# Second parts of feed-forward weights and activations: accumulating transfers in place of GpSimd subtractions

## The chip, the cores and the metric

The kernel runs on one core of a Trainium2 chip. The metric is the device time of one execution in microseconds (us); lower is better. The engines named below are TensorE (PE, with its weight load PEld), VectorE (DVE), ScalarE (ACT), GpSimd (POOL) and SyncE (SP, which issues transfers).

## The reference, cut to what matters

One inference step of a one-layer decoder trunk on 512 prompt rows and 64 sample rows, 576 tokens in all, with a model width of 1024. A token mixing part (a chunked state space recurrence beside a delta-rule recurrence) comes first. The change lies in the feed-forward block behind it:

```python
h = h + mix
hf = rmsnorm(h, w['norm_ffn'])
h = h + (jax.nn.silu(hf @ w['w_gate']) * (hf @ w['w_up'])) @ w['w_down']
gate = jax.nn.sigmoid(rmsnorm(h, w['norm_ple']) @ w['w_ple_gate'])
h = h + gate * (p.astype(h.dtype) @ w['w_ple_proj'])
```

All data are float32, and `D_FF` is 2816, which is 22 tiles of 128 columns.

## The kernel before, in words

**Two parts for every operand.** The matmuls take operands of a rounded float32 type. So every weight tile and every activation tile is kept as a first part `hi`, its rounded copy, and a second part `lo = source - hi`. A product is then formed as three matmul groups: hi by hi, hi by lo, lo by hi. `split` (L185) makes the two parts of a tile in SBUF, `wsplit` (L197) loads a weight tile of 128 x 512 from HBM into `raw` first. In both, ACT writes `hi` with a copy, and DVE or GpSimd writes `lo` with a subtraction (L194, L206). Which of the two does it is told by `lo_eng`, by `only`, or by a counter `flip` that alternates between GpSimd and DVE.

**Buffers.** `raw` has three buffers, `whi` and `wlo` of `wsplit` have two each (pool `wp`). A buffer of `raw` is free when its second part has been formed; one of `whi` or `wlo` when PE has done the matmuls that read it.

**The feed-forward stage** (L1355 on) goes over the 22 column tiles in eleven pairs.
- Pair one (loop `for f in range(2)`) uses plain linear layers: `linear` (L225) reads a tile of four 128-row weight blocks with `wload` and issues 24 matmuls of 288 columns for it (four blocks, two halves of the tokens, three groups). With the order `WLAST` the second part of the weight comes last.
- Pairs two to eleven (loop `for p in range(1, NFF // 2)`, p from 1 to 10) form the gate projection of both tiles with seven block products in place of eight (`gate_pair`, L1411). It loads the weight blocks a11, a21, a22 and a12, forms the sums s1, s2 and s4 on DVE (tile `sw`) and one difference on GpSimd (L1418), and calls `product` (L1399) seven times. Each `product` splits its weight into `wh` and `wl` (three buffers each) and issues twelve matmuls: first part by both parts of the activation, then second part by the first part. The results are put together by DVE (L1431, L1437, L1440) and GpSimd (L1429, L1434, L1435), and go through Silu on ACT.
- For each tile of a pair an up projection follows (`linear`, two weight tiles), DVE multiplies it onto the gate, and `inner` splits the result into `ah` and `al`, the activations of the down projection.
- After pair six (p = 5) and after pair eleven (p = 10) `down` (L1446) multiplies what has been collected by `w_down`: eight `linear` calls of three weight tiles each, whose results DVE scales and GpSimd adds to `h` (L1452).

The activation operands T1 to T4 of the block products are formed once, ahead of pair two (L1375 to L1388), by DVE, ACT and GpSimd.

**The order.** Each engine runs its instructions in the order in which they were laid out when the program was built; a planner that simulates the times of the instructions (`schedule_with_timeline_sim=True`) chooses that order, starting from the order of the source. SP issues all weight loads, in order too. The kernel before issues no transfer from GpSimd.

Of the kernel before, what the change touches and what calls it, by code (L numbers as in the profile page):

```python
# [8 lines left out]
F32 = mybir.dt.float32  # L9
F32R = mybir.dt.float32r  # L10
AF = mybir.ActivationFunctionType
ALU = mybir.AluOpType
# [63 lines left out]
def hybrid_step(ctx, tc, A):  # L76
# [2 lines left out]

    cp = ctx.enter_context(tc.tile_pool(name="cp", bufs=1))  # L80
    wp = ctx.enter_context(tc.tile_pool(name="wp", bufs=2))
    xp = ctx.enter_context(tc.tile_pool(name="xp", bufs=8))
    lin = ctx.enter_context(tc.tile_pool(name="lin", bufs=2, space=PSUM))
    dp = ctx.enter_context(tc.tile_pool(name="dp", bufs=1, space=DRAM))
# [3 lines left out]
    def nm(s):  # L88
        uid[0] += 1
        return f"{s}_{uid[0]}"  # L90

    def act(out, in_, func=AF.Copy, scale=1.0, bias=0.0):
        return S.activation(out, in_, func, bias=bias, scale=scale)  # L93
# [87 lines left out]
    wat = [0]  # L181
    flip = [0]
    only = [None]

    def split(src, pool, tags, shape, lo_eng=None, hi=None, lo=None, hi_eng=None, **kw):  # L185
        hi = hi if hi is not None else pool.tile(shape, F32R, tag=tags[0], name=nm(tags[0]), **kw)
        lo = lo if lo is not None else pool.tile(shape, F32R, tag=tags[1], name=nm(tags[1]), **kw)
        if hi_eng:
            hi_eng.tensor_copy(hi[:], src)
        else:  # L190
            act(hi[:], src)
        flip[0] += 1
        eng = lo_eng or (G if flip[0] % 2 else V)
        eng.tensor_tensor(lo[:], src, hi[:].bitcast(F32), ALU.subtract)  # L194
        return hi, lo

    def wsplit(src, n, hi=None, lo=None):  # L197
        raw = wp.tile([P, 512], F32, tag="raw", name=nm("raw"), bufs=3)
        nc.sync.dma_start(raw[:, 0:n], src)
        if hi is None:  # L200
            hi = wp.tile([P, 512], F32R, tag="whi", name=nm("whi"))
            lo = wp.tile([P, 512], F32R, tag="wlo", name=nm("wlo"))
        act(hi[:, 0:n], raw[:, 0:n])
        flip[0] += 1
        eng = only[0] or (G if flip[0] % 2 else V)
        eng.tensor_tensor(lo[:, 0:n], raw[:, 0:n], hi[:, 0:n].bitcast(F32), ALU.subtract)  # L206
        return hi, lo

    ahead = []
# [1136 lines left out]

    XF = st["x"]
    AF2 = []

    def inner(s_):  # L1350

        f = len(AF2)
        AF2.append(split(s_[:], fp, (f"ah{f}", f"al{f}"), [P, NT], lo_eng=G))

    for f in range(2):  # L1355
        ps = lin_ps()
# [42 lines left out]
    def product(ps, w, n, first, eng):  # L1399
        hi, lo = split(w[:], cm, ("wh", "wl"), [P, 512], lo_eng=eng, bufs=3)  # L1400
        for p, q in WLAST:
            for k in range(4):
                T.matmul(ps, (hi, lo)[p][:, k * P:(k + 1) * P], OPS[n][k][q], start=first and p == q == k == 0,  # L1403
                         stop=p == 1 and k == 3, skip_group_check=True)
# [6 lines left out]
    def gate_pair():  # L1411
# [10 lines left out]
        sa, sb = ft("sa"), ft("sb")  # L1422
        product(a, a11, "B11", True, V)
        p1 = kept(a)
        product(b, s2, "T2", True, G)
        p6 = kept(b)
        product(c, s1, "T1", True, V)
        p5 = kept(c)
        G.tensor_tensor(p6[:], p6[:], p1[:], ALU.add)  # L1429
        product(a, a12, "B21", False, G)  # L1430
        V.tensor_tensor(sa[:, N1], a, rs[:, N1], ALU.mult)  # L1431
        product(b, a21, "T3", False, V)
        p67 = kept(b)
        G.tensor_tensor(p67[:], p67[:], p1[:], ALU.add)  # L1434
        G.tensor_tensor(sb[:, N2], p67[:], p5[:], ALU.add)  # L1435
        product(c, s4, "B22", False, G)
        V.tensor_tensor(sa[:, N2], c, p6[:], ALU.add)  # L1437
        V.tensor_tensor(sa[:, N2], sa[:, N2], rs[:, N2], ALU.mult)
        product(b, a22, "T4", False, V)
# [15 lines left out]
        AF2.clear()  # L1455

    for p in range(1, NFF // 2):
        for s_ in gate_pair():
            up = lin_ps()
            linear(XF, up, WLAST)  # L1460
            V.tensor_tensor(s_[:], up, s_[:], ALU.mult)
            inner(s_)
        if p == NSPLIT - 1:
            down(False)
# [208 lines left out]
```

## Time and profile before

| | us |
|---|---|
| median of three runs | 1341.91 |
| lowest, highest | 1338.66, 1345.79 |
| span of the profiled execution | 1349.0 |

The profile is of one execution, and its page gives its span, from the first to the last instruction, and no other time for it. A row of the profile names the engine, the operation, the tile written and the tiles read ("wlo<-raw,whi" is the second part of a weight tile, "al<-sa,ah" that of an activation), the count, the busy time in us and the mean of one in ns. "Idle before" is the time in which the engine stood still ahead of these instructions, and what ended it. A view by stretches of time gives each engine's busy time in the stretch, the clock that was granted to PE (1.00 is full speed) and the share of time in which the 16 DMA engines were busy.

### The profile page before, as it was taken

Reading aid. Unit: us, or ns where it says so; the run is one execution under the profiler, and the core shown is the slowest. Engines: PE = TensorE matmul, PEld = TensorE weight load, DVE = VectorE, ACT = ScalarE, POOL = GpSimd, SP = SyncE. Lnnn points to the kernel's source line nnn. Section 1 sums busy time; section 2 is a strip of 40 time slices with the busy share of each in tenths; the row PEclk is TensorE's granted clock in tenths of the full one; section 3 lists DMA queues with packets and bytes.
Section 4 is the critical chain, followed back from the end, with each engine's and each line's share of the span. In section 5 each row is a group of like instructions: output and inputs, shape, how many; then the busy total and the mean of one; then the engine's idle time right before and its main releaser. Section 6 shows DMA issues by size and latency. Waiting matters only on the chain.

```text
span 1349.0 us, 26596 instructions
## 1 busy us (share of the span) xinstructions
PE 1246.8 (92%) x10525; PEld 1150.7 (85%) x10525; DVE 826.0 (61%) x1443; ACT 618.9 (46%) x1256; POOL 625.6 (46%) x597
## 2 busy tenths in 40 slices
PE   6897999999989978899999969989999999999997
PEld 6787897889868957788779859889999999999997
DVE  6648666887687785943466667886553135443454
ACT  6565436534654463343434364464442124433363
POOL 5425413642355154122456645565654336654642
PEclk9897799899979978889989989998999999999998
DMA  5322242234232412262454542222323222314322
GB/s 164 125 68 66 77 117 63 85 103 116 75 99 78 109 41 80 94 214 83 157 176 131 179 125 72 73 93 88 92 88 87 79 86 82 93 59 149 96 89 71
DMA packets 94461, 135.58 MB, mean 100 GB/s; under 512 B 34705, under 2 KB 39057, under 8 KB 94337
## 3 DMA queue, kind: packets, MB, share of 16 engines
q1 hardware_dynamic: 93760, 133.36, 32.4%
q8 instruction: 83, 1.36, 0.4%
q10 hardware_dynamic: 576, 0.52, 0.1%
q14 instruction: 42, 0.34, 0.1%
HBM read 106.10 MB, written 27.75 MB: 99 GB/s over the span
## 4 chain that ended last, share of the span: by engine, by line
PE 63%; DVE 14%; ACT 4%; issue 4%; DMA 3%; POOL 3%; DVEq 0%; SPq 0%; ACTq 0%; POOLq 0%
PE lin L234 21%; PE lin L1403 8%; PE lin L223 6%; PE lin L221 6%; PE lin L222 6%; DVE h L395 2%; PE lin L1508 1%; PE lin L1509 1%; PE lin L1510 1%; DVE tmp L674 1%; DVE wlo L206 1%; DVE Tt L676 1%; PE lin L613 1%; PE cx L797 1%; DVE suv L831 1%
## 5 line engine op out<-in xcount | busy, mean ns | idle before, releaser
L206 POOL TENSOR_TENSOR wlo<-raw,whi 128x512 fp32r<-128x512 f32 (+1 forms) x108 | 146.4, 1356 | 352.5 <-ACT whi L93 269.5
L93 ACT ACTIVATE whi<-raw 128x512 fp32r<-128x512 f32 (+1 forms) x232 | 143.3, 618 | 259.1 <-PE lin L234 126.4
L221 PE MATMUL lin<-xhi,whi 128*128 128x288 f32 (+1 forms) x784 | 243.3, 311 | 2.5 <-ACT whi L93 2.2
L223 PE MATMUL lin<-xhi,wlo 128*128 128x288 f32 (+1 forms) x784 | 241.5, 308 | 2.3 <-POOL wlo L206 2.3
L222 PE MATMUL lin<-xlo,whi 128*128 128x288 f32 (+1 forms) x784 | 241.5, 308 | 0.3 <-POOL xlo L194 0.3
L206 DVE TENSOR_TENSOR wlo<-raw,whi 128x512 fp32r<-128x512 f32 (+1 forms) x124 | 100.9, 814 | 103.2 <-PE lin L234 60.4
L221 PEld LDWEIGHTS lin<-xhi,whi 128*128 128x128 f32 (+1 forms) x784 | 151.0, 193 | 9.3 <-ACT whi L93 2.6
L223 PEld LDWEIGHTS lin<-xhi,wlo 128*128 128x128 f32 (+1 forms) x784 | 150.7, 192 | 6.2 <-POOL wlo L206 2.8
L222 PEld LDWEIGHTS lin<-xlo,whi 128*128 128x128 f32 (+1 forms) x784 | 150.8, 192 | 4.8 <-issue 1.2
L234 PE MATMUL lin<-xhi,whi 128*128 128x288 f32 x384 | 62.3, 297 | 3.2 <-ACT xhi L93 3.0
L234 PE MATMUL lin<-xlo,whi 128*128 128x288 f32 x384 | 60.8, 298 | 0.0
L234 PE MATMUL lin<-xhi,wlo 128*128 128x288 f32 x384 | 59.3, 297 | 0.0
L234 PEld LDWEIGHTS lin<-xhi,whi 128*128 128x128 f32 x384 | 54.6, 189 | 3.8 <-ACT xhi L93 1.7
L234 PEld LDWEIGHTS lin<-xlo,whi 128*128 128x128 f32 x384 | 54.8, 191 | 0.0
L234 PE MATMUL lin<-ah,wlo 128*128 128x288 f32 x352 | 54.7, 296 | 0.0
L234 PE MATMUL lin<-al,whi 128*128 128x288 f32 x352 | 54.7, 296 | 0.0
L234 PE MATMUL lin<-ah,whi 128*128 128x288 f32 x352 | 54.7, 296 | 0.0
L234 PEld LDWEIGHTS lin<-xhi,wlo 128*128 128x128 f32 x384 | 54.3, 191 | 0.0
L1403 PE MATMUL lin<-T,wh 128*128 128x288 f32 x320 | 50.1, 296 | 4.5 <-DVE T L194 2.8
L674 DVE TENSOR_TENSOR tmp<-L,Tt 72x30 f32<-72x30 f32 (+14 forms) x120 | 49.2, 410 | 3.2
L234 PEld LDWEIGHTS lin<-ah,whi 128*128 128x128 f32 x352 | 49.6, 189 | 0.0
L234 PEld LDWEIGHTS lin<-ah,wlo 128*128 128x128 f32 x352 | 49.6, 189 | 0.0
(425 smaller groups left out, 3197.8 us busy)
## 6 DMA issues: line engine op xcount, KB each, us to landing
raw<-wts SPq DMA_DIRECT2D x271, 256.0 KB, 2.6
S<-s_wkv SPq DMA_DIRECT2D x8, 512.0 KB, 5.1
hd<-s_ssm SPq DMA_DIRECT2D x8, 512.0 KB, 4.5
o_ssm_s<-hd SPq DMA_DIRECT2D x8, 512.0 KB, 2.9
xbc_d<-E SPq DMA_DIRECT2D x12, 288.0 KB, 2.1
x<-xT SPq DMA_DIRECT2D x8, 288.0 KB
gate_d<-g SPq DMA_DIRECT2D x8, 288.0 KB, 2.5
bv_d<-rw SPq DMA_DIRECT2D x8, 288.0 KB
```

What stands on the lines that cost most here:

```text
L93: return S.activation(out, in_, func, bias=bias, scale=scale)
L206: eng.tensor_tensor(lo[:, 0:n], raw[:, 0:n], hi[:, 0:n].bitcast(F32), ALU.subtract)
L221: T.matmul(ps[:, a:b], whi, xhi[:, a:b], start=first, stop=False)
L222: T.matmul(ps[:, a:b], whi, xlo[:, a:b], start=False, stop=False)
L223: T.matmul(ps[:, a:b], wlo, xhi[:, a:b], start=False, stop=last)
L234: T.matmul(ps[:, a:e], (hi, lo)[p][:, i * P:(i + 1) * P], xs[k + i][q][:, a:e], start=n == k + i == 0, stop=n == 2 and k + i == nk - 1, sk ...
L395: V.scalar_tensor_tensor(h[:], E[:, i:i + 600], w(i), h[:], ALU.mult, ALU.add)
L613: T.matmul(ps[:, c:c + 128].rearrange("p (a t) -> p a t", a=2), s.BK[jj][H[e], g].rearrange("p a t -> p (a t)"), s.G[H[e], g, jj, :, e], s ...
L674: V.tensor_tensor(o, L[:, jx:jx + 1, jx + 1:32].to_broadcast([NB, jx, n]), Tt[:, 0:jx, jx:jx + 1].to_broadcast([NB, jx, n]), ALU.mult)
L676: V.tensor_tensor(Tt[:, 0:jx, jx + 1:32], Tt[:, 0:jx, jx + 1:32], o, ALU.subtract)
L797: T.matmul(uw[H[e], jj, :], TT[H[e], g, jj, :], xs[H[e], jj, :], start=True, stop=True)
L1403: T.matmul(ps, (hi, lo)[p][:, k * P:(k + 1) * P], OPS[n][k][q], start=first and p == q == k == 0, stop=p == 1 and k == 3, skip_group_check ...
```

## The change

For pairs three to ten the second parts that GpSimd formed are formed in another way: ACT writes the negated copy of the source into `lo` (rounded like the first part, so it is the negated first part), and then GpSimd issues a transfer from the source to `lo` with accumulation, which leaves source minus first part. This is `below` with the engine "D". `side` holds "D" from p = 2 to p = 9 and GpSimd otherwise; it goes to the second product (s2), the fourth (a12), to `inner`, and to every other weight tile in `wsplit`. The sixth product (s4) uses "D" in pairs two to eleven. What DVE subtracts stays with DVE.

From the start of the feed-forward stage `whi` and `wlo` come from a new pool `wq` with three buffers each; the two buffers of each in `wp` stay for the stages before. The space that is reserved in SBUF for the descriptors of GpSimd's transfers is set to 1024 bytes.

```diff
+    wq = ctx.enter_context(tc.tile_pool(name="wq", bufs=1))
...
+    side, wide = [G], [None]
+
+    def below(lo, src, hi, eng):
+
+        if eng == "D":
+            act(lo, src, scale=-1.0)
+            G.dma_start(lo, src, accum_op=ALU.add)
+        else:
+            eng.tensor_tensor(lo, src, hi.bitcast(F32), ALU.subtract)
...
-        eng = lo_eng or (G if flip[0] % 2 else V)
-        eng.tensor_tensor(lo[:], src, hi[:].bitcast(F32), ALU.subtract)
+        below(lo[:], src, hi[:], lo_eng or (G if flip[0] % 2 else V))
         return hi, lo
...
-            hi = wp.tile([P, 512], F32R, tag="whi", name=nm("whi"))
-            lo = wp.tile([P, 512], F32R, tag="wlo", name=nm("wlo"))
+            pool, bufs = wide[0] or (wp, 2)
+            hi = pool.tile([P, 512], F32R, tag="whi", name=nm("whi"), bufs=bufs)
+            lo = pool.tile([P, 512], F32R, tag="wlo", name=nm("wlo"), bufs=bufs)
         act(hi[:, 0:n], raw[:, 0:n])
         flip[0] += 1
-        eng = only[0] or (G if flip[0] % 2 else V)
-        eng.tensor_tensor(lo[:, 0:n], raw[:, 0:n], hi[:, 0:n].bitcast(F32), ALU.subtract)
+        below(lo[:, 0:n], raw[:, 0:n], hi[:, 0:n], only[0] or (side[0] if flip[0] % 2 else V))
         return hi, lo
...
+    wide[0] = (wq, 3)
...
-        AF2.append(split(s_[:], fp, (f"ah{f}", f"al{f}"), [P, NT], lo_eng=G))
+        AF2.append(split(s_[:], fp, (f"ah{f}", f"al{f}"), [P, NT], lo_eng=side[0]))
...
-        product(b, s2, "T2", True, G)
+        product(b, s2, "T2", True, side[0])
...
-        product(a, a12, "B21", False, G)
+        product(a, a12, "B21", False, side[0])
...
-        product(c, s4, "B22", False, G)
+        product(c, s4, "B22", False, "D")
...
     for p in range(1, NFF // 2):
+        side[0] = "D" if 1 < p < NFF // 2 - 1 else G
...
-    nc = _bacc.Bacc("TRN2", target_bir_lowering=False, num_devices=1)
+    nc = _bacc.Bacc("TRN2", target_bir_lowering=False, num_devices=1, dynamic_dma_scratch_size=1024)
```

## The prediction

> **What bounds the kernel now.** The page's first lines say that TensorE is the busiest engine.
>
> ```profile
> span 1349.0 us, 26596 instructions
> ## 1 busy us (share of the span) xinstructions
> PE 1246.8 (92%) x10525; PEld 1150.7 (85%) x10525; DVE 826.0 (61%) x1443; ACT 618.9 (46%) x1256; POOL 625.6 (46%) x597
> ```
>
> That is a mean over stages. The change lies in the feed-forward stage, so next I read the stretches of that stage: its entry (900 to 926), pairs two to six (926 to 1018), the first down projection (1018 to 1097), pairs seven to eleven (1097 to 1214), the last down projection (1214 to 1274). The columns are length, then busy time and count of PE, PEld, DVE, ACT and POOL, the granted clock, and the DMA engines' share and rate.
>
> ```profile
> 900.00:911.00 11.00, 6.74 (x47) 5.98 (x45) 10.79 (x14) 6.37 (x14) 8.34 (x8) 0.98 0.11 34
> 911.00:926.00 15.00, 14.55 (x87) 14.32 (x87) 6.90 (x13) 5.49 (x11) 4.27 (x4) 0.79 0.27 82
> 926.00:1018.00 92.00, 91.97 (x693) 92.00 (x694) 55.17 (x66) 42.14 (x76) 61.91 (x46) 1.00 0.30 89
> 1018.00:1097.00 79.00, 79.00 (x595) 79.00 (x594) 17.26 (x23) 17.08 (x27) 31.20 (x23) 1.00 0.29 84
> 1097.00:1214.00 117.00, 117.00 (x884) 117.00 (x883) 60.17 (x74) 49.42 (x89) 69.85 (x53) 1.00 0.27 79
> 1214.00:1274.00 60.00, 60.00 (x452) 60.00 (x451) 19.62 (x27) 21.80 (x36) 31.49 (x24) 1.00 0.40 122
> ```
>
> From 926 to 1274 PE is full at the full granted clock: 92.00 us / 693 = 132.8 ns for each 288-column matmul, 117.00 / 884 = 132.4 ns later. A busy PE could still be waiting inside, so I ask for PE's waits, from 850 to 930:
>
> ```profile
> PE lin L234 <- ACT xhi L93: 3.0, 2, 1.7
> PE lin L1403 <- DVE T L194: 2.8, 1, 2.8
> PE lin L1403 <- ACT T L93: 1.7, 2, 1.0
> PE lin L234 <- DVE sa L1461: 0.2, 1, 0.2
> ```
>
> The last row is the stall of 0.2 us at 926; behind it, up to 1274, the same view has none. So pairs three to ten, which the change rewrites, **run at PE's rate and have nothing to give**. GpSimd's subtractions there are beside PE, not in front of it.
>
> **The change part by part.** Removed from GpSimd, by its groups between 926 and 1274:
>
> ```profile
> L206 POOL TENSOR_TENSOR wlo<-raw,whi 128x512 fp32r<-128x512 f32 x37 | 48.9, 1321 | 77.8 <-ACT whi L93 40.1 <-PE lin L234 23.2 <-issue 14.5
> L194 POOL TENSOR_TENSOR wl<-sw,wh 128x512 fp32r<-128x512 f32 x18 | 26.4, 1466 | 15.3 <-ACT wh L93 15.3
> L1452 POOL TENSOR_TENSOR h<-h,dn 128x576 f32<-128x576 f32 x15 | 24.5, 1634 | 16.2 <-DVE dn L1451 16.2
> L194 POOL TENSOR_TENSOR al<-sa,ah 128x576 fp32r<-128x576 f32 x10 | 18.0, 1797 | 0.9 <-ACT ah L93 0.9
> L194 POOL TENSOR_TENSOR al<-sb,ah 128x576 fp32r<-128x576 f32 x10 | 14.8, 1482 | 5.9 <-ACT ah L93 5.9
> L194 POOL TENSOR_TENSOR wl<-raw,wh 128x512 fp32r<-128x512 f32 x9 | 12.6, 1398 | 6.2 <-ACT wh L93 6.2
> L1418 POOL TENSOR_TENSOR raw<-raw,raw 128x512 f32<-128x512 f32 x9 | 12.2, 1353 | 26.6 <-DVE sw L1416 26.6
> L1435 POOL TENSOR_TENSOR sb<-e,e 128x288 f32<-128x288 f32 x10 | 12.1, 1210 | 0.0
> L1434 POOL TENSOR_TENSOR e<-e,e 128x288 f32<-128x288 f32 x9 | 10.9, 1209 | 0.0
> L1429 POOL TENSOR_TENSOR e<-e,e 128x288 f32<-128x288 f32 x9 | 8.6, 960 | 0.0
> ```
>
> Each of the eight pairs turns seven second parts into transfers: two wl from sw, one wl from raw, two al, two of its four wlo (the alternation with DVE stays). The first down projection adds 12 of its 24 wlo, and the s4 of pairs two and eleven one each: 8 x 7 + 12 + 2 = **70 transfers**. Off GpSimd go 28 x 1.32 + 18 x 1.47 + 8 x 1.40 + 16 x 1.64 = 101 us, and 70 issues come on. On the path to the end this is worth 0.
>
> Added to ACT: 70 negated copies of the size of the first part's.
>
> ```profile
> L93 ACT ACTIVATE whi<-raw 128x512 fp32r<-128x512 f32 x74 | 46.6, 630 | 114.3 <-PE lin L234 91.7 <-issue 13.3 <-POOL e L1429 4.9
> ```
>
> 54 x 0.63 plus 16 wider ones at 0.68 make 45 us. By the stretches ACT is busy 42 + 17 + 49 = 108 of the 288 us from 926 to 1214, so 153 fit. Cost 0; the cover is ACT's idle time, most of which is waiting for PE to free a first-part buffer. Without that cover they would cost up to 45 us.
>
> Added to the DMA engines: the transfers. None like them is in this trace, so their **latency** is bounded by the nearest rows, a 256 KB load and a 512 KB load (KB, then us from issue to landing):
>
> ```profile
> raw<-wts SPq DMA_DIRECT2D x271, 256.0 KB, 2.6
> S<-s_wkv SPq DMA_DIRECT2D x8, 512.0 KB, 5.1
> ```
>
> An accumulate reads 256 KB twice and writes it once. As one load it takes 2.6 us; as 768 KB on the line through the two rows, 2.6 + 2 x 2.5 = 7.6 us. I take 5.1, the row with the two reads' bytes. With the copy, a second part is ready 0.63 + 5.1 = 5.7 us after its buffer is free (bounds 3.2 to 8.2), before GpSimd's own issue time. The Trainium skill ("DMA: Bandwidth & Descriptors", Anatomy of one DMA) fits a GpSimd transfer as 2.0 us plus its bytes over 436 GB/s: by it, an estimate of 3.8 us for 768 KB, which leaves the sum as it is; no run here shows it yet.
>
> How long can PE wait for it? The tightest place is the down projection, where PE does nothing but weight tiles. PE in order of time (start, length):
>
> ```profile
> 1025.34 1.23 PE L234 MATMUL lin<-ah,wlo 128*128 128x288 f32 x8
> 1026.40 1.23 PE L234 MATMUL lin<-ah,whi 128*128 128x288 f32 x8
> 1027.47 1.23 PE L234 MATMUL lin<-al,whi 128*128 128x288 f32 x8
> 1028.54 1.23 PE L234 MATMUL lin<-ah,wlo 128*128 128x288 f32 x8
> 1029.61 1.23 PE L234 MATMUL lin<-ah,whi 128*128 128x288 f32 x8
> 1030.67 1.23 PE L234 MATMUL lin<-al,whi 128*128 128x288 f32 x8
> 1031.74 1.23 PE L234 MATMUL lin<-ah,wlo 128*128 128x288 f32 x8
> ```
>
> A wlo buffer is free when its last matmul ends (1025.34 + 1.23 = 1026.57) and with two buffers is read again at 1031.74: 5.2 us. The change gives these tiles three buffers, one tile of 3.2 us (1029.61 - 1026.40) more: **8.4 us, against 5.7**. The upper bound, 8.2, just fits. In the pairs wh and wl have three buffers before and after:
>
> ```profile
> 954.62 0.69 PE L1403 MATMUL lin<-T,wl 128*128 128x288 f32 x4
> ...
> 964.18 0.69 PE L1403 MATMUL lin<-T,wl 128*128 128x288 f32 x4
> ```
>
> These are three products apart: free at 955.31, read at 964.18, 8.9 us. So the latency is hidden, cost 0. One place is not: the last al of pair six, whose ah is done at 1021.86 + 0.69 = 1022.55
>
> ```profile
> 1021.86 0.69 ACT L93 ACTIVATE ah<-sb 128x576 fp32r<-128x576 f32 x1 [0.82 <-DVE sb L1461]
> ```
>
> and which the last two of the eight matmuls at 1027.47 read, 0.8 us on, at 1028.27. That gives 5.7 us for 0.68 + 5.1 = 5.8: **+0.1 us**, once (0 to 2.6).
>
> **GpSimd's issue time** is not shown either. SP's row for two issues is
>
> ```profile
> 953.66 1.48 SPq L1395 DMA_DIRECT2D raw<-wts  x2
> ```
>
> so 0.74 us each there; a subtraction takes 1.32 to 1.80. I take 1.3, no change for what queues behind it (the sums of e, raw and sb, and h). A pair lasts 180 matmuls x 132.7 ns = 23.9 us, and what stays on GpSimd is 1.35 + 1.21 + 1.21 + 0.96 = 4.7 us, so GpSimd becomes the bound only over (23.9 - 4.7) / 7 = **2.7 us an issue**.
>
> Bandwidth: from 926 to 1214 the share is 0.29 at 84 GB/s, some 24 MB. Seventy accumulates write 18 MB; counted once to three times they add 0.22 to 0.65, at most 0.94 in all. Here the Trainium skill speaks against the change (same page, Issuing engines are not separate DMA queues): the issuing engine does not matter, all transfers share 16 engines and interleave. The shares are what would show it; the estimate by it is the same sum plus slower raw loads, whose tiles are loaded ahead.
>
> Three wlo buffers also act at the stage's entry, before the transfers begin. There PE stood still for 2.8 us:
>
> ```profile
> 907.14 1.34 PE L1403 MATMUL lin<-T,wh 128*128 128x288 f32 x9
> 911.25 0.61 PE L1403 MATMUL lin<-T,wh 128*128 128x288 f32 x1 [2.76 <-DVE T L194]
> ```
>
> A third weight tile ready could fill the hole with its first 16 matmuls, 16 x 132.7 ns = 2.1 us of later work. Bounds: 0, as the releaser is DVE's T chain, not a weight; at most the waits of 3.0 + 2.8 + 1.7 us and the slow clock behind them (87 matmuls in 14.55 us instead of 11.5, 3.0 us), 10.5 us. I take **-2.1**, since the place is certain and DVE's chain (10.79 of 11 us busy) stays.
>
> **Sum:** -2.1 + 0.1 = -2.0 us. The profiled span is 1349.0 us, 7.1 above the median of the runs, so I carry only the difference: 1341.9 - 2.0, about **1340**.
>
> **Rivals.**
> - *The entry closes* (faster): all of the 10.5 us is won, 1341.9 - 10.5 = 1331. For it: clock 0.79 behind the hole. Against: the three long waits are for x and T, which the change does not form. Chance 0.12.
> - *Landing late* (slower): chain and issue together exceed 8.4 us in the down projection and 8.9 in the pairs, because transfer and raw loads crowd each other. Every other tile is a transfer and each stall gives the next one its time, so half the excess is paid: at 10.5 us that is 12 x 2.1 / 2 = 13 us there and 24 products x 1.6 / 2 = 19 us in the pairs, 32 us: 1374. It decides from 8.4 us. Against it: the taken 5.7. Chance 0.14.
> - *GpSimd becomes the bound* (slower): over 2.7 us an issue; at 3.5 us, 7 x 8 x 0.8 = 45 us: 1387. Chance 0.07.
> - *In-order queues* (slower): ACT's copy waits for PE to free a second-part buffer, and e, Silu and the next first part stand behind it; 0.15 us on each of 70 is 10 us: 1352. Chance 0.07.
> - *The change does not relieve GpSimd*: an issue takes as long as its subtraction. Then the time is the forecast's, and it is in that case.
>
> **How the numbers follow.** The forecast has 0.60. It is the case within 0.5% of the median (6.7 us, about what a measurement of this kernel can tell from no change); its own range is 1336 to 1347. Faster is the first rival, 0.12; slower the next three, 0.28. For 8 in 10 the range runs from 1331, the whole entry, to 1374, the late landing at 10.5 us; GpSimd as the bound is left out.
>
> **What would show it.** Right: PE still at 132 to 133 ns a matmul from 926 to 1214 with no waits on wlo, wl or al; GpSimd's busy time down by about 100 us, ACT's up by 45; landing of the accumulates under 7 us. Wrong: PE waits released by a DMA in the down projection (late landing), GpSimd without gaps between issues over 2.7 us long (the bound), a granted clock under 1.00 after such waits. The forecast falls if issue plus landing is over 7.8 us.

## The result, and the profile after

| | before | after |
|---|---|---|
| median of five runs each, us | 1345.79 | 1359.64 |
| lowest, highest, us | 1338.66, 1346.97 | 1352.93, 1362.42 |
| ratio | | 1.0101, 95% interval 1.0068 to 1.0135 |
| span of the profiled execution, us | 1349.0 | 1353.3 |

The changed kernel is slower by about one per cent; no change was forecast. The two spans differ by only 4.3 us, while the medians differ by 13.9. So I first look for a measure that is taken inside the stage. The view of one tile gives the first and the last start of its instructions. Before:

```profile
L1451 DVE TENSOR_TENSOR dn<-lin,rstd x16: 757/758/758, 1029.8 to 1280.4; 128x576 f32<-128x576 f32 x16
```

```profile
L1431 DVE TENSOR_TENSOR sa<-lin,rstd x10: 457/458/459, 919.5 to 1204.2; 128x288 f32<-128x288 f32 x10
```

After:

```profile
L1461 DVE TENSOR_TENSOR dn<-lin,rstd x16: 752/757/758, 1029.3 to 1283.5; 128x576 f32<-128x576 f32 x16
```

```profile
L1441 DVE TENSOR_TENSOR sa<-lin,rstd x10: 457/458/459, 911.7 to 1207.9; 128x288 f32<-128x288 f32 x10
```

From the first `sa` product of pair two to the last `dn`, in which all but two of the 70 transfers lie, **before took 1280.4 - 919.5 = 360.9 us and after 1283.5 - 911.7 = 371.8**. That is 10.9 us more. This distance, called the *pair stretch* below, is the measure of all the experiments: a program that is run again repeats it to 0.1 us, while the part ahead of it moves by several us from one execution to the next (the two other profiles of the kernel before reach the same mark at 913.2 and 912.5, not 919.5).

Where do the 10.9 us lie? The page's line of busy times after:

```profile
PE 1246.2 (92%) x10525; PEld 1148.4 (85%) x10525; DVE 806.9 (60%) x1443; ACT 653.1 (48%) x1326; POOL 586.6 (43%) x597
```

The stretches after (the columns are those of before):

```profile
926.00:1018.00 92.00, 90.07 (x677) 89.59 (x676) 39.56 (x60) 51.20 (x97) 40.83 (x43) 1.00 0.70 158
1018.00:1097.00 79.00, 78.81 (x592) 78.58 (x591) 16.57 (x24) 24.48 (x39) 23.43 (x21) 1.00 0.55 131
1097.00:1214.00 117.00, 113.89 (x855) 113.19 (x854) 49.62 (x71) 61.17 (x115) 51.60 (x51) 1.00 0.64 144
```

GpSimd is relieved (625.6 to 586.6 us) and ACT loaded (618.9 to 653.1), as the change means to. The down projection, 1018 to 1097, stays full. But in the pairs PE issues 677 matmuls in 92 us where it issued 693, and 855 in 117 us where it issued 884 (the stretches are cut at the same times, not at the same work). The DMA engines' share went from 0.30, 0.29 and 0.27 to 0.70, 0.55 and 0.64. What PE waited for, from 905 to 1290 (us in total, times, longest):

```profile
PE lin L1413 <- DMA wl<-sw: 3.0, 3, 1.7
PE lin L243 <- DVE sa L1472: 2.6, 1, 2.6
PE lin L1413 <- DMA wl<-raw: 2.0, 2, 1.2
PE lin L1413 <- DVE T L193: 1.4, 2, 0.9
PE lin L349 <- DVE rn L346: 0.4, 1, 0.4
PE lin L243 <- DMA al<-sb: 0.2, 1, 0.2
```

Before, PE waited only 0.2 us behind the entry. Now five waits, 5.0 us, end with the landing of a `wl`, and one of 2.6 us at the entry (at 920.8) with DVE's `sa`. The matmuls behind a hole run slower at first. Behind the one at the entry eight took 1.92 us (1.22 elsewhere), the clock granted to PE from 921 to 926 was 0.66, and 1.6 us were lost beside the wait; behind each of the shorter holes it was 0.3 us or less. Added up over the pair stretch, PE's holes make 7.8 us (0.2 before) and the slower matmuls behind them 3.4 (0.2 before): together 10.8 of the 10.9 us. None of the waits ends with a `wlo`, and 0.2 us with an `al`. So the transfers that are late are those of the block products. They are not slow as a rule: their issue and landing (the last column is the median in us from issue to landing):

```profile
raw<-wts SPq DMA_DIRECT2D x113, 256.0 KB, 2.8
wlo<-raw POOLq DMA_DIRECT2D x28, 256.0 KB, 4.1
wl<-sw POOLq DMA_DIRECT2D x18, 256.0 KB, 4.0
al<-sa POOLq DMA_DIRECT2D x8, 288.0 KB, 3.8
al<-sb POOLq DMA_DIRECT2D x8, 288.0 KB, 4.7
...
wl<-raw POOLq DMA_DIRECT2D x8, 256.0 KB, 5.5
```

One stall shows what stands in front of such a transfer. From the changed kernel's timelines of ACT, of GpSimd and of PE:

```profile
970.67 0.69 ACT L94 ACTIVATE sb<-sb 128x576 f32<-128x576 f32 x1 [1.39 <-DVE sb L1451]
971.26 0.62 ACT L94 ACTIVATE wh<-raw 128x512 fp32r<-128x512 f32 x1
971.79 0.39 ACT L94 ACTIVATE e<-lin 128x288 f32<-128x288 f32 x1
972.18 0.69 ACT L94 ACTIVATE ah<-sb 128x576 fp32r<-128x576 f32 x1
972.77 0.67 ACT L94 ACTIVATE al<-sb 128x576 fp32r<-128x576 f32 x1
973.35 0.61 ACT L94 ACTIVATE wl<-raw 128x512 fp32r<-128x512 f32 x1
```

```profile
974.09 0.86 POOL L191 DMA_DIRECT2D al<-sb  x1 [3.83 <-ACT wl L94]
974.79 1.04 POOL L191 DMA_DIRECT2D wl<-raw  x1
```

```profile
969.70 0.69 PE L1413 MATMUL lin<-xhi,wl 128*128 128x288 f32 x4
...
980.17 0.79 PE L1413 MATMUL lin<-xhi,wl 128*128 128x288 f32 x4 [0.76 <-DMA wl<-raw]
```

The copy into `wl` at 973.35 has four others ahead of it on ACT, all behind a Silu that waited for DVE. On GpSimd the transfer of `al`, which nobody needs before the down projection at 1018, goes first. From the issue of `wl` to PE's start there are 980.17 - 974.79 = 5.4 us.

The first row of PE gives the whole account. It is the product of a11, three products earlier, so its `wl` buffer is the one that is filled here, and it came free at 969.70 + 0.69 = 970.39. Until the copy began 3.0 us went by (973.35), from there to the issue 1.4 (974.79), and from the issue to PE 5.4: **9.8 us, where the prediction had 8.9 to spend and counted 5.7**. With a copy that starts at once it would have been 6.8 us. From the start of the copy to the landing the 26 `wl` took 4.2 to 7.9 us, 5.3 in the median, so by itself this chain, the one that the prediction counted, stayed under 8.9 every time.

Why 5.4, when a transfer can be quicker? The view of `wlo` in the first down projection, 1030 to 1096, where transfers are mostly alone, and then the view of `wl` from 926 to 1284:

```profile
DMA to landing us min/median/max: 3.3/3.3/4.3
```

```profile
DMA to landing us min/median/max: 3.3/4.3/6.7
```

Sorted by how many of GpSimd's transfers are under way with the one just issued, the trace gives for all 70:

```
under way   transfers   median us to landing (lowest to highest)
1           32          3.37 (3.25 to 4.37)
2           19          4.47 (3.32 to 7.38)
3           19          5.21 (4.06 to 6.66)
```

There are never four. The weight loads add to it: where less than a quarter of a 256 KB load moved in the first 3.3 us of a transfer, the medians for one, two and three under way are 3.3, 3.8 and 4.8 us, and where three quarters or more moved, 3.7, 4.4 and 5.6. So the products' transfers land late where others, and loads, are on the way with them.

### The profile page after: what moved, and what is told of

Same layout as the page of the kernel before. It is cut to its first block, busy times and chain, and to the rows that moved or that the text cites. A ratio compares the mean times of both kernels' runs of the same rounds, so it can differ in the third digit from the quotient of the medians.

```text
span 1353.3 us, 26772 instructions
## 1 busy us (share of the span) xinstructions
PE 1246.2 (92%) x10525; PEld 1148.4 (85%) x10525; DVE 806.9 (60%) x1443; ACT 653.1 (48%) x1326; POOL 586.6 (43%) x597
## 5 line engine op out<-in xcount | busy, mean ns | idle before, releaser
L193 POOL TENSOR_TENSOR wlo<-raw,whi 128x512 fp32r<-128x512 f32 (+1 forms) x80 | 107.9, 1349 | 295.7 <-ACT whi L94 238.9
L193 DVE TENSOR_TENSOR wlo<-raw,whi 128x512 fp32r<-128x512 f32 (+1 forms) x124 | 93.4, 754 | 107.4 <-ACT whi L94 58.0
L243 PEld LDWEIGHTS lin<-xhi,wlo 128*128 128x128 f32 x384 | 54.7, 189 | 0.0
L243 PE MATMUL lin<-ah,wlo 128*128 128x288 f32 x352 | 54.7, 296 | 0.0
L191 POOL DMA_DIRECT2D wlo<-raw x28 | 26.7, 954 | 56.8 <-ACT wlo L94 39.8
L1413 PEld LDWEIGHTS lin<-T,wh 128*128 128x128 f32 x320 | 45.3, 189 | 5.7 <-ACT T L94 3.6
```

The lines of the kernel that those rows point to most:

```text
L191: G.dma_start(lo, src, accum_op=ALU.add)
L193: eng.tensor_tensor(lo, src, hi.bitcast(F32), ALU.subtract)
L243: T.matmul(ps[:, a:e], (hi, lo)[p][:, i * P:(i + 1) * P], xs[k + i][q][:, a:e], start=n == k + i == 0, stop=n == 2 and k + i == nk - 1, sk ...
```

## The experiments

Each diff is against the changed kernel, unless said otherwise, and the letters of the theories are those of the expectation beside them. A planner lays out the queues anew for every edit, so single stalls move; what counts is the pair stretch and the kind of wait.

**The kernel before, once more**, in two groups of runs, both times without any edit.

> The kernel before itself, as a control: a second profile, and a ratio that must be 1.000 within its interval if the runs can tell half a per cent. Stage 418 us as in the first profile. What is asked is the front (from the start to the first matmul of the feed-forward stage): 862.3 us in the first profile of before, 854.8 to 859.3 in all five kernels with the new pool, whose instructions there are the same. If the front varies by execution, it is somewhere from 850 to 862 here and its differences say nothing.

> The kernel before, unchanged, once more beside these: ratio 0.999 to 1.001, 360.9 us from the first sa product of pair two to the last dn. It gives the spread against which the small differences of the others (0.997 to 1.0045 for kernels whose stage is unchanged) are read.

Measured: 1.0001 (0.9978 to 1.0023) and 0.9976 (0.9957 to 0.9996); pair stretch 360.9 and 360.8 us. The same program differs from itself by a quarter of a per cent, which is more than the second interval allows. A ratio between 0.997 and 1.003 therefore proves nothing here; the pair stretch is the sharper tool.

**The reserved space alone**: the kernel before with

```diff
+    nc = _bacc.Bacc("TRN2", target_bir_lowering=False, num_devices=1, dynamic_dma_scratch_size=1024)
```

> The kernel before with only the descriptor space set to 1024 bytes, which moves tiles to other addresses. Theory F (the front pays some 3 to 6 us for other addresses, which is why the kernel with only third buffers is 0.45% slower with a stage of 418.0 us): time 1.003 to 1.005. Theory G (there is no such cost, or it comes from the new pool): time 0.998 to 1.002. Stage 416 to 419 in both.

Measured: 360.8 us, 0.9972 (0.9952 to 0.9993). No cost; and no gain that is proved, since the unchanged kernel came to 0.9976.

**No transfers, but the new buffers and space.**

```diff
-        product(c, s4, "B22", False, "D")
+        product(c, s4, "B22", False, G)
...
-        side[0] = "D" if 1 < p < NFF // 2 - 1 else G
+        side[0] = G
```

> The new pool with three buffers for whi and wlo and the smaller descriptor space stay; every second part that the change made a transfer goes back to GpSimd's subtraction. Call the stage the time from the first matmul of the feed-forward stage to the last scaling of a down projection (the first start of an xhi,whi matmul to the last start of a dn): 418.1 us in the kernel before (862.3 to 1280.4), 426.9 in the changed one (856.6 to 1283.5). Theory A (the transfers hold the source tiles until they land, weight loads come late, and the queues that run in order pass it on to PE): no transfers, no loss; stage 416 to 418, no PE waits on a DMA, time 0.995 to 1.000 of the kernel before. Theory B (the second parts themselves come late for PE's ring of wh and wl): the same, 416 to 418. Theory C (ACT's extra copies): the same. Theory D (the new order that the planner makes with three buffers costs the time): stage 424 or more, time 1.005 or more.

Measured: 361.0 us, no new waits; ratio 1.0045 (1.0025 to 1.0065). The buffers do not cost anything in the stage. Where the four tenths of a per cent lie in the runs no profile shows; that stays open.

**ACT's copies without the transfers**: GpSimd adds the source instead.

```diff
-            G.dma_start(lo, src, accum_op=ALU.add)
+            G.tensor_tensor(lo, src, lo.bitcast(F32), ALU.add)
```

> ACT's negated copies stay, 70 of them, but GpSimd adds the source to them in place of the transfer, so nothing is in flight and a source is free when GpSimd has added it. Theories A and B: the loss is gone, stage 416 to 419, no PE wait on a DMA, time within 0.4% of the kernel before. Theory C (the copies on ACT's queue are the cost): stage 424 or more, time 1.006 or more.

Measured: 361.4 us, 1.0024 (1.0003 to 1.0045). All 70 copies together cost 0.5 us; alone they are hidden.

**More source buffers.** A source (`raw`) is now held until its transfer has landed, which could hold back the loads. Four and then five `raw` buffers (with five, `whi` has two):

```diff
-        raw = wp.tile([P, 512], F32, tag="raw", name=nm("raw"), bufs=3)
+        raw = wp.tile([P, 512], F32, tag="raw", name=nm("raw"), bufs=5)
...
-            hi = pool.tile([P, 512], F32R, tag="whi", name=nm("whi"), bufs=bufs)
+            hi = pool.tile([P, 512], F32R, tag="whi", name=nm("whi"), bufs=2)
...
-        t = pool.tile([P, 512], F32, tag=tag, name=nm(tag), bufs=3)
+        t = pool.tile([P, 512], F32, tag=tag, name=nm(tag), bufs=5 if pool is wp else 3)
```

> The changed kernel with four raw buffers in place of three, for the whole program. Theory A: the weight loads get one more source tile to run ahead of the transfers; SP's waits on a landing wlo fall from 118 us to under 70, ACT's waits on a raw load from 29 us to under 12, PE's stalls in the pairs from 8.9 us to under 5, stage 418 to 423. Theory B: the ring of wh and wl is as long as before, PE's waits on wl stay at 5 us or more, stage 425 to 428.

> The changed kernel with five raw buffers, and whi back at two to make room (wlo stays at three). Theory A: the loads are never late, ACT's waits on a raw load under 6 us, PE's stalls under 3 us, stage 416 to 420, time within 0.4% of the kernel before. Theory B: PE's waits on wl stay at 5 us or more, stage 425 to 428, time 1.006 or more.

Measured: 368.6 us and 1.0107 (1.0087 to 1.0127) with four; 370.8 us and 1.0092 (1.0070 to 1.0114) with five. The loads do come earlier: ACT's first parts of plain tiles wait for them 4.9 us with four and not at all with five, in place of 29.1. But the loss stays. With five, all of PE's waits in the pairs, from 915 on, end with a landing:

```profile
PE lin L1413 <- DMA wl<-raw: 3.7, 2, 2.4
PE lin L1413 <- DMA wl<-sw: 2.0, 2, 1.5
```

So the held sources are not the whole of it. One of these stalls, from the timelines of ACT, of GpSimd and of PE of the kernel with five:

```profile
948.49 0.64 ACT L94 ACTIVATE wl<-sw 128x512 fp32r<-128x512 f32 x1
```

```profile
949.21 0.88 POOL L191 DMA_DIRECT2D al<-sb  x1 [0.40 <-ACT wl L94]
949.78 1.15 POOL L1439 TENSOR_TENSOR e<-e,e 128x288 f32<-128x288 f32 x1
950.53 1.25 POOL L191 DMA_DIRECT2D wl<-sw  x1
```

```profile
957.03 0.80 PE L1413 MATMUL lin<-xhi,wl 128*128 128x288 f32 x4 [1.46 <-DMA wl<-sw]
```

The copy into `wl` ends at 949.13; `al` and `e` are ahead on GpSimd until 950.53; then 6.5 us to landing. **From the start of the copy to PE there are 8.5 us, where the prediction took 5.7**, and that leaves 0.4 of its 8.9 us for whatever stands ahead of the copy. The transfers around it, with the landings that the trace has for them:

```
issued   landed   transfer
942.00   947.64   al<-sa
942.55   948.90   wlo<-raw
945.27   950.16   wlo<-raw
947.95   952.09   wl<-raw     0.31 behind the landing of the third before it
949.21   955.03   al<-sb      0.31
950.53   956.99   wl<-sw      0.37
```

Three in a row are issued just when the third transfer before them has landed. In the eight kernels with 54 transfers or more there are never more than three under way, and in seven of them some issue follows such a landing by 0.31 to 0.32 us, the least distance that occurs. GpSimd's queue is held by that: the copies behind the issues at 945.27 and 947.95 had ended 3.0 and 3.2 us before.

**One more wl buffer** (four, with `wh` still three and `whi` two).

```diff
+        lo = cm.tile([P, 512], F32R, tag="wl", name=nm("wl"), bufs=4)
-        hi, lo = split(w[:], cm, ("wh", "wl"), [P, 512], lo_eng=eng, bufs=3)
+        hi, lo = split(w[:], cm, ("wh", None), [P, 512], lo_eng=eng, lo=lo, bufs=3)
```

> The changed kernel with four wl buffers in place of three for the block products (whi goes back to two to make room, wlo stays at three, raw at three). Theory B (a second part by transfer comes later than the ring of three wl allows, 8.9 us): PE's waits on wl, 5.0 us and 3.9 to 5.6 us in the kernels with more raw, fall under 1.5 us, PE's stalls from 8.9 us to under 4.5 us, stage 419 to 423. Theory A (held source tiles) or crowding of the transfers whatever the ring: waits on wl stay at 3.5 us or more, stage 425 or more.

Measured: 370.4 us, 1.0071 (1.0044 to 1.0097). Little is won: PE's waits on `wl` are 6.1 us, where theory B had under 1.5. But this edit can't tell the theories apart: ACT fills `wh` ahead of `wl` in the same queue, and `wh` still had three buffers. Four of both are tried below.

**One kind of transfer at a time.** Plain tiles only (28 `wlo`), block products only (26 `wl`), activations only (16 `al`), and all but the activations (54):

```diff
-        below(lo[:, 0:n], raw[:, 0:n], hi[:, 0:n], only[0] or (side[0] if flip[0] % 2 else V))
+        below(lo[:, 0:n], raw[:, 0:n], hi[:, 0:n], only[0] or (G if flip[0] % 2 else V))
...
-        AF2.append(split(s_[:], fp, (f"ah{f}", f"al{f}"), [P, NT], lo_eng=side[0]))
+        AF2.append(split(s_[:], fp, (f"ah{f}", f"al{f}"), [P, NT], lo_eng=G))
```

Both edits leave the products; the second alone leaves all but the activations; for the other two the products get `G` in place of `side[0]` and `"D"`.

> Transfers only for the 28 wlo of the plain linear layers; the block products' wl and the activations' al go back to GpSimd's subtraction. Theory B: no PE wait on a DMA, stage 416 to 420, all the loss of the stage is gone. Theory A: these 28 hold the raw buffers of the weight loads, so SP's waits on a landing wlo stay near 118 us and some half of the loss stays, stage 421 to 424.

> Only the 26 wl of the block products are accumulating transfers; the activations' al and the plain tiles' wlo stay subtractions. From the first sa product of pair two to the last dn TensorE took 360.9 us before and 371.8 with all 70 transfers. Theory P (the block products' wl are what TensorE waits for, because copy, GpSimd queue and landing exceed the 8.9 us that three buffers give): this kernel shows most of it, 365 to 371 us, with 3 to 8 us of TensorE waits released by DMA landings of wl; ratio 1.005 to 1.010. Theory C (crowding: only all kinds of transfers together are too much): landing of wl stays near 4 us, 361 to 362.5 us, under 1 us of such waits; ratio 0.998 to 1.003.

> Only the 16 al of the activations are accumulating transfers (16 of 288 KB); wl and wlo stay subtractions. Theory P: al is needed only at the down projections, so 361 to 362 us from the first sa product of pair two to the last dn (360.9 before, 371.8 after), at most 0.5 us of TensorE waits on al at the first down projection; ratio 0.998 to 1.003. If the al transfers cost by themselves (through what they delay in GpSimd's queue: sums of e and sb): above 364 us, waits on DVE or GpSimd.

> The 26 wl and the 28 wlo are transfers; the 16 al are GpSimd subtractions again (1.48 to 1.80 us each in GpSimd's queue in place of 0.9 us of issue). Theory P: the loss stays, 367 to 372 us from the first sa product of pair two to the last dn, TensorE waits on wl of 4 to 9 us; ratio 1.006 to 1.011. Theory A (an al transfer of 288 KB that stands just ahead of a wl transfer in the same queue is what makes that wl land late): the waits go, under 363 us, wl landing near 4 us; ratio under 1.004.

| transfers | pair stretch, us | against 360.9 | ratio (interval) |
|---|---|---|---|
| plain tiles only | 361.3 | +0.4 | 1.0005 (0.9983 to 1.0026) |
| activations only | 361.0 | +0.1 | 1.0029 (1.0008 to 1.0050) |
| products only | 364.8 | +3.9 | 1.0056 (1.0028 to 1.0083) |
| products and plain tiles | 370.5 | +9.6 | 1.0100 (1.0063 to 1.0138) |
| all | 371.8 | +10.9 | 1.0101 (1.0068 to 1.0135) |

Without the products' `wl` the transfers are free. The activations add little, so the `al` ahead of `wl` in GpSimd's queue is not what decides. But the parts do not add up: 3.9 and 0.4 by themselves become 9.6 together. The crowd of three is not what it takes either: products and plain tiles together have only 3 of their 54 transfers issued as the third under way, and none of them right behind a landing (1.8 us at the least), and yet nearly all of the loss. And with products only, where at most two are under way, the expected waits on landings did not come; PE's waits in the pairs are mainly

```profile
PE lin L1413 <- ACT wh L94: 1.7, 2, 1.5
PE lin L1413 <- DVE wl L193: 0.7, 2, 0.5
```

released by the in-order engines ahead of the transfer.

**Four buffers of both wh and wl**, products only, and the same rings without any transfer.

```diff
-    wide[0] = (wq, 3)
+    wide[0] = (wq, 2)
...
-        hi, lo = split(w[:], cm, ("wh", "wl"), [P, 512], lo_eng=eng, bufs=3)
+        hi, lo = split(w[:], cm, ("wh", "wl"), [P, 512], lo_eng=eng, bufs=4)
```

> Only the 26 wl of the block products are transfers, as in the kernel with products only, and wh and wl both have four buffers (whi and wlo of the plain tiles two each, as before the change). Products only, with three: 364.8 us from the first sa product of pair two to the last dn, against 360.9 before; from the sa product of the second tile of pair two on 347.0 against 344.3. Theory B (the budget: copy, GpSimd queue and landing together outlast three products, 8.9 us; one more product, 2.9 us, covers them): 344.3 to 345 us behind that second mark, no TensorE waits on wl over 0.3 us; ratio at or under 1.004. Theory Q (the in-order queues: copies, sums and transfers that stand behind one another start late whatever the number of buffers): 346.5 to 348, waits on wh or wl of 2 us or more; ratio 1.004 to 1.008.

> No transfers: the kernel before with the small reserved space, four buffers of wh and wl and two of whi and wlo. If longer rings are worth something by themselves (the entry's hole of 2.8 us closes in part): under 358 us from the first sa product of pair two to the last dn or under 415 us from the first matmul of the stage, ratio under 0.998. If they only serve the transfers: 360.5 to 361.5 us, ratio 0.997 to 1.003.

Measured: 360.6 us with the 26 transfers, 1.0007 (0.9982 to 1.0032), no wait of PE on `wl` in the stretch but the end of one of 1.4 us that lies across its first mark. The second mark of the expectation gave 346.1 in place of 344.3 to 345, but only because that mark itself comes earlier in the new order (14.5 us behind the first instead of 16.5); the whole stretch is what it was before. The same rings without transfers: 363.0 us, 1.0013 (0.9989 to 1.0037), so some 2 us of any such difference can come from the planned order alone. Counted from the first matmul of the stage, so that the mark can't move, it is 421.8 us for products only with three buffers, 417.1 with four, 417.6 with four and no transfers, and 415.5 to 418.1 in the three profiles of the kernel before. With that allowance, **the products' 3.9 us go with a longer ring**: with products alone, three buffers were what was too short.

**Do the plain tiles add by their transfers or by ACT's copies?** The 26 `wl` by transfer, the plain tiles by copy and addition, the activations by subtraction.

```diff
+        elif eng == "C":
+            act(lo, src, scale=-1.0)
+            G.tensor_tensor(lo, src, lo.bitcast(F32), ALU.add)
...
-        below(lo[:, 0:n], raw[:, 0:n], hi[:, 0:n], only[0] or (side[0] if flip[0] % 2 else V))
+        below(lo[:, 0:n], raw[:, 0:n], hi[:, 0:n], only[0] or (("C" if side[0] == "D" else G) if flip[0] % 2 else V))
```

> The 26 wl are transfers; the 28 wlo that the change makes transfers get ACT's negated copy and an addition on GpSimd in place of a transfer. Transfers alone in the products took 364.8 us from the first sa product of pair two to the last dn, transfers in products and plain tiles 370.5. Theory C (crowding: 28 more transfers on the shared DMA engines and in GpSimd's queue lengthen the landing of wl): this kernel stays at 364 to 366.5, wl landing median under 4.1 us. Theory Q (ACT's 28 more copies in its in-order queue hold back wh, wl and e): 368.5 to 371.5, with TensorE waits released by wl or ACT of 5 us or more.

Measured: 367.6 us, 1.0080 (1.0053 to 1.0106), between the two theories. From 364.8 the 28 copies make 2.8 us more, and their transfers another 2.9 (370.5). Each step is little above what the order alone can do, but where they lie is plain. The 2.8 us are the entry's hole (`sa L1475`, 2.5 us): between the two `sa` products of pair two there are 21.1 us, against 17.7 with products only, and behind them 346.5 against 347.0. So the copies cost nothing in the pairs behind. With the plain tiles as transfers it is 21.4 and 349.2, so these do cost something there. The entry's hole does not need them.

**Pair two without its transfer** (and pair eleven without its own).

```diff
-        product(c, s4, "B22", False, "D")
+        product(c, s4, "B22", False, side[0])
```

> The changed kernel with the s4 of pairs two and eleven subtracted by GpSimd again: 68 transfers, none issued before pair three. With all 70 the stretch between the two sa products of pair two took 21.2 us against 16.5 before, and the rest of the stage 350.6 against 344.3. Theory E (the entry's hole comes from the transfer in pair two, whose wl lands late and whose source buffer is held, so that the loads of pair three start late): 16.5 to 17.3 us between those two marks, 350 to 351 behind them; ratio 1.005 to 1.009. Theory O (the hole comes from the order of the queues that goes with transfers in the pairs behind, not from this one): 19.5 to 21.5 us there; ratio 1.008 to 1.012.

Measured: 17.8 us between the two marks in place of 21.2, so that hole all but goes, but 357.9 behind them in place of 350.6; 375.7 in all, 1.0116 (1.0070 to 1.0161). Neither sum came true. The hole is not the transfer's alone: the kernels with four `wl`, with products only and with five `raw` have that transfer too, and 17.8, 17.7 and 18.5 us there. It goes with the order that the planner chose, and taking it away wins nothing: the stalls come up again later.

**All 70 transfers with the longer ring** (four `wh` and `wl`), with three and with two `wlo`.

> All 70 transfers of the change, with four buffers of wh and wl in place of three (whi two, wlo three). Theory B (the products' ring of three is what is too short): the loss of the changed kernel goes, 360.5 to 363 us from the first sa product of pair two to the last dn in place of 371.8 (360.9 before), TensorE waits on wl under 1.5 us together; ratio 0.999 to 1.004. Theory Q (landing and queues of 70 transfers together are too much for any ring that fits): 365 us or more, waits on wl of 3 us or more; ratio over 1.005.

> As the kernel with four wh and wl and all 70 transfers, but with two buffers of wlo. By the prediction's count a wlo buffer is then read again 5.2 us after it is free, and copy and landing take 0.6 + 4.1 us and GpSimd's issue 0.9, 5.6 us together. Theory B holds for this ring too: the first down projection, 67.2 us from its first dn to its eighth so far, gets waits on wlo, 0.2 to 1 us for each of 12 transfers with part of it passed on: 69 to 75 us. If 67.2 to 68 us: the third wlo buffer was not needed and the count is too strict.

Measured: 373.5 us, 1.0098 (1.0069 to 1.0127), and 376.9 us, 1.0102 (1.0079 to 1.0125). So the cure of the products alone does not cure the change: theory B falls for it. With three `wlo` PE now waits, from 905 to 1290, twice as long for DVE as for landings:

```profile
PE lin L1413 <- DVE sa L1447: 3.6, 1, 3.6
PE lin L1413 <- DMA wl<-sw: 3.0, 4, 1.4
PE lin L1413 <- DVE sa L1441: 2.6, 3, 1.1
```

What DVE stands for is seen in its order of time:

```profile
955.40 0.69 DVE L1426 TENSOR_TENSOR sw<-raw,raw 128x512 f32<-128x512 f32 x1 [5.05 <-DMA raw<-wts]
956.01 0.69 DVE L193 TENSOR_TENSOR wlo<-raw,whi 128x512 fp32r<-128x512 f32 x1
956.61 1.78 DVE L1427 TENSOR_TENSOR sw<-sw,raw 128x512 f32<-128x512 f32 x1
958.31 0.45 DVE L1441 TENSOR_TENSOR sa<-lin,rstd 128x288 f32<-128x288 f32 x1
```

A `sw` sum waits 5 us for a late load, and the `sa` that PE needs stands behind it. DVE's waits for loads, from 905 to 1290, are 34.5 us in nine waits there, against 4.7 in seven before and 7.6 in eight after:

```profile
DVE sw L1426 <- DMA raw<-wts: 34.5, 9, 6.6
```

Only a part of this is the held source. The kernel with the same rings and no transfers has 18.5 us of these waits, in nine, at a ratio of 1.0013; the other 16 come with the transfers. SP issues its loads in order: ahead of the load that DVE waited for, from 933 to 951, it had waited 6.2 us for the landing of a `wl`, 2.3 for landings of `wlo`, and 5.8 and 0.6 for subtractions of DVE.

With two `wlo` the first down projection, from its first `dn` to its eighth, took 73.0 us in place of 67.3, inside the expected 69 to 75, but not for the expected reason. Between these marks PE did 32 matmuls of block products, where the kernel before had 3; 29 matmuls at 0.133 us are 3.9 of the 5.7 us, and that is the planner's order. PE waited for a `wlo` once, 1.5 us, and the other eleven transfers came in time. So this run neither bears out nor refutes the prediction's count of 5.2 us with two buffers.

**What this settles.** The transfers are the cause: without them, with or without ACT's copies, the loss is gone, and without those of the products too. A transfer holds more than GpSimd did: its destination for the wait on ACT, the copy, the queue and the landing, and its source until it has landed. For the products alone that was too much for rings of three, and rings of four cured it. With the plain tiles as transfers too, landings with others under way take longer, loads come late behind held sources, and the copy into `wl` starts late on ACT; then four `wl` are not enough (3.0 us of waits left). Most of the loss is there with hardly any third transfers, no held issues and no transfers of activations. Five `raw` take away the waits on DVE and leave those on `wl`; four `wl` leave both. How the loss of the full change splits between the entry, the landings and ACT's queue can't be told from these runs, since every edit also changes the planned order. Five `raw` with four `wh` and `wl` were not tried, so that the full change could be made free stays open. So does what sets the limit of three. The reserved space of 1024 bytes is the suspect: the Trainium skill ("SBUF — State Buffer", SBUF size: 192, 224, or 256?) names the space as the ring of descriptors of GpSimd's transfers and gives 16 KiB of each partition for it. No run here had transfers with more than 1024 bytes.

## Why the prediction failed

- **GpSimd's relief, 101 us, worth 0.** Right. GpSimd went from 625.6 to 586.6 us, which is 101 less and about 62 more for 70 issues of 0.87 to 0.99, and the time did not gain.
- **GpSimd's issue, taken as 1.3 us, bound from 2.7.** The issues took less, and the rival of GpSimd as the bound is out:

```profile
L191 POOL DMA_DIRECT2D wlo<-raw x27 | 25.7, 952 | 55.8 <-ACT wlo L94 39.8 <-DVE dn L1461 11.0 <-DVE sb L1472 4.0
...
L191 POOL DMA_DIRECT2D wl<-sw x16 | 14.0, 876 | 3.2 <-issue 1.7 <-ACT wl L94 1.0 <-PE lin L243 0.2
```

- **70 copies on ACT, 45 us, cost 0.** Right for the copies alone (0.5 us with additions in place of transfers). The 28 copies beside the products' transfers cost nothing behind the entry either. But the cover, ACT's idle time, was read as free time for the copy that is needed next, and in an order that is laid out beforehand it is not: `wl` at 973.35 stood behind four others and a wait.
- **Latency taken as 5.1 us, bounds 2.6 to 7.6.** The medians were 3.8 to 5.5, so the size was too high for most and too low for the slowest. The Trainium skill's fit ("DMA: Bandwidth & Descriptors", Anatomy of one DMA), an estimate of 3.8 us for 768 KB, is near `wl<-sw` (4.0) and `wlo` (4.1), but not `wl<-raw` (5.5), and above the 3.3 of transfers that are mostly alone.
- **"So the latency is hidden, cost 0", in the pairs. This is the step that failed.** It set 0.63 + 5.1 = 5.7 us, a copy and one latency for every transfer, against 8.9 from the moment when the buffer is free. As a typical chain from the copy on, 5.7 was right (5.3 in the median). Two things failed. The copy was taken to start as soon as the buffer is free, so the time ahead of it, in ACT's queue, stood at nothing: in the stall added up above it was 3.0 us. And the latency was taken as a constant: it was 3.4 us alone, 5.2 with three under way, up to 6.7 for a `wl`. GpSimd's queue, which the text named and left out ("before GpSimd's own issue time"), took another 0.8 us there. In that stall 3.0 + 0.6 + 0.8 + 5.4 us came together; without the first term, or with a landing of 3.4 us, it would have fitted into 8.9. Two other stalls, of 1.2 and 0.2 us, came behind a `whi` that held ACT for a late load, 4.4 and 4.1 us, with `wh`, `e` and `wl` behind it; the longest, 1.7 us, had the longest landing, 6.7. The first of the two behind a `whi`:

```profile
1002.10 0.63 ACT L94 ACTIVATE whi<-raw 128x512 fp32r<-128x512 f32 x1 [4.40 <-DMA raw<-wts]
1002.63 0.62 ACT L94 ACTIVATE wh<-sw 128x512 fp32r<-128x512 f32 x1
1003.16 0.69 ACT L94 ACTIVATE e<-lin 128x288 f32<-128x288 f32 x2
1003.74 0.63 ACT L94 ACTIVATE wl<-sw 128x512 fp32r<-128x512 f32 x1
```

  PE has no slack, so it pays for the late tiles, and the early ones give nothing back.
- **The same step in the down projection.** Right: 67.0 us from its first `dn` to its eighth against 67.3 before, no waits on `wlo`. There the transfers come one by one, 6.4 us apart, and land in 3.3. Whether the third `wlo` buffer was needed for it stays open: with two, and another order, PE waited 1.5 us for one of the twelve.
- **The last al of pair six, +0.1 us.** Right: PE waited 0.2 us for `al<-sb`.
- **Raw loads cost nothing, "whose tiles are loaded ahead".** Wrong: a source is held until the transfer lands. ACT's first parts of plain tiles waited 29.1 us for loads, none before, and DVE's `sw` sum 7.6 instead of 4.7. Taking these waits away with more `raw` did not take away the loss, though.

```profile
L94 ACT ACTIVATE whi<-raw 128x512 fp32r<-128x512 f32 x72 | 45.3, 629 | 108.5 <-PE lin L243 66.1 <-DMA raw<-wts 29.1 <-PE lin L1413 8.0
```

- **DMA share up by 0.22 to 0.65.** Right: up by 0.26 to 0.40.
- **The entry, -2.1 us.** It can't be told apart from the spread of executions: from the first matmul of the stage to the first `sa` there are 55.1 us after the change, and 57.3, 54.7 and 54.7 in the three profiles of the kernel before. And another hole, of 2.6 us until DVE's `sa`, opened behind it; with the slower matmuls that followed it cost 4.2 us.
- **The rivals.** What came is nearest to "landing late": one of its two places (the pairs, not the down projection), its point (8.9 us) and, in part, its cause (transfers and loads crowd each other), at some 10 us in place of 32. It was given 0.14, since the taken chain of 5.7 spoke against it. The other part is "in-order queues", with the roles exchanged: it had the copy hold back what stands behind it, and here the copy was the one held back. The two rivals came as one, and their chances should have been read together. Of the signs of being wrong, PE waits in the down projection did not come (0.2 us for an `al`), as the waits were in the pairs; the granted clock under 1.00 behind a wait came at the entry, 0.66. (The forecast's own range, 1336 to 1347, is a little narrower than the 0.5% of the median that it names, 1335 to 1349.)

## What to carry to other kernels

Compare the buffers' budget with the worst chain, not the typical one, and start it where the buffer comes free: everything ahead on each in-order engine on the way, the copy, the issue, and a landing under the new load. An operation that becomes a transfer holds its source as well as its destination until it lands, so both rings have to be counted. When PE is full at its own rate, relieving another engine can win nothing, and any new chain that is sometimes late can only lose.

## What had not been expected of the hardware

An accumulating transfer of 256 KB within SBUF lands 3.3 us after its issue when it is alone, and 5.2 us after it, in the median, as the third under way. There were never more than three of GpSimd's transfers under way, and the next was issued 0.31 us after a landing at the earliest. GpSimd was busy 0.88 to 0.96 us for each issue of 256 KB, against 1.32 to 1.47 us for the subtraction that it replaced. Ten holes of PE over 2 us, 2.2 to 3.6, lie in the pair stretches of the changed kernel and its variants; behind each the next matmuls lost another 1.6 us at a lowered clock (0.66 from 921 to 926 in the changed kernel). And the same program, run again, came to 0.9976 of itself.
